# Start of a transformer-step kernel reordered: conv constants, modulation loads and bias tables on other places of their queues

## The chip, the cores and the metric

The kernel runs on one core of one Trainium2 chip. The metric is device microseconds of one execution, as the median of several runs. TensorE (PE in the rows) does the matmuls, VectorE (DVE), ScalarE (ACT) and GpSimd (POOL) work beside it, and SyncE (SP) issues nearly all DMAs. Each engine works through its own instructions in a fixed order.

## The reference

One layer of a streaming encoder step, on 2048 prompt rows and 8 x 16 sample rows of width 1024. Two head groups run side by side on one projection:

```python
sh1, sc1, g1, sh2, sc2, g2 = modulation(c, w_mod, b_mod)      # silu(c) @ w_mod + b_mod, in six parts
h = rmsnorm(x, norm1_g) * (1 + sc1) + sh1
proj = h @ w_in
o_a, conv_state, s = mixer_a(proj, conv_left, s0, conv_w, ...)  # conv of width 4 on q/k/v, gated delta rule
qb = rmsnorm(proj[..., QB:KB], qn_g); kb = rmsnorm(proj[..., KB:VB], kn_g); vb = proj[..., VB:]
o_b = band attention of qb, kb, vb with rel_bias on clipped distances
x = x + g1 * (concat(o_a, o_b) @ w_out)
h = rmsnorm(x, norm2_g) * (1 + sc2) + sh2
x = x + g2 * (relu(h @ w_up) ** 2 @ w_down)
```

w_mod is 1024 x 6144; all is float32. Before a row of x can be projected, the parts shift1 (section 0) and scale1 (section 1) of the modulation must be known.

## The kernel before

Each product is made of three matmuls (`mm3`, L160): a value is split into a high part, rounded to fp32r, and a low part, the rest. `weights` (L166) loads a tile of a weight matrix into a buffer `raw` (three of them), lets ScalarE cast it into the high half of a buffer `w` (four of them, L175), and GpSimd subtract to get the low half (L180). For w_in in the first block of rows the low half is then stored in DRAM (s_w_in, L183), and each later block loads it from there (L178) instead of subtracting.

Phase 1 goes over six blocks of rows: block 0 is two prompt tiles of 128 rows and the sample tile, blocks 1 to 4 have three tiles, block 5 two. `proj_a` makes of each block the gates of group A (PSUM tile psg; two loads of w_in, L0 and L1 in the prediction), then q, k, v (psq; one load of w_in for each of 12 sections, 24 matmuls of up to 384 columns), then the other half of the gates. `proj_b` makes q, k, v of group B (psb, 12 loads). Between them small steps of the delta rule are put in as fill; the projection of group B for blocks 5, 4 and 2 comes last, with the first attention block as fill. Phase 2 is attention, w_out, w_up and w_down.

Ahead of block 0 stands `modulation_start` (L220). It loads sections 1 and 0 of w_mod in 16 pieces of 512 KB through nine buffers raw0, sums each with `mod_mm` (psum tile mps), adds b_mod, and turns the sum by a matmul with `sel` (ptm) into the columns modT. On the way it loads the three x tiles of block 0, each after four sums. After its loop come `conv_consts` (three pairs of small loads, 24 transposes) and `load_hT`, which normalises x, transposes it (psh), scales it with modT and splits it into hT, the input of all projections. hT's columns 0 to 511 need quarters 0 and 1 of the sections only, the others quarters 2 and 3.

The other four sections of w_mod are 32 pieces, one loaded by `mod_step` (L272) after each q/k/v section from block 1 on; so they are loaded in blocks 1, 2 and two thirds of 3. `rel_bias` (L1090) writes the reversed bias table s_ext to DRAM and copies it out to s_bias (8 x 128 rows of 640 floats) and s_bs, from DRAM to DRAM; s_bias is first read by the attention behind block 5.

All DMAs named here stand in SyncE's one queue. The order on each engine is not the order of the code: a list scheduler places each instruction when the program is built, in each engine's order, and the chip keeps to it.

## Time and profile before

| what | value |
|---|---|
| median of 3 runs | 3190.09 us (3189.9 to 3201.82) |
| the profiled execution | 3191.66 us |
| its span in the trace | 3190.0 us, 53098 instructions |
| PE busy | 3060.4 us (96%) |
| DVE, ACT, POOL busy | 1768.1, 1471.8, 593.5 us |
| block 0 (first gate matmul to the start of block 1) | 46 to 203 us |

The profile is of one execution. A busy PE is not PE at its peak, since matmuls overlap and their ends are modelled. In a timeline row the bracket at the end is the idle time of the engine before that instruction, and what released it.

### The profile page before, as it was taken

Reading aid. Unit: us, or ns where it says so; the run is one execution under the profiler, and the core shown is the slowest. Engines: PE = TensorE matmul, PEld = TensorE weight load, DVE = VectorE, ACT = ScalarE, POOL = GpSimd, SP = SyncE. Lnnn points to the kernel's source line nnn. Section 1 sums busy time; section 2 is a strip of 40 time slices with the busy share of each in tenths; the row PEclk is TensorE's granted clock in tenths of the full one; section 3 lists DMA queues with packets and bytes.
Section 4 is the critical chain, followed back from the end, with each engine's and each line's share of the span. In section 5 each row is a group of like instructions: output and inputs, shape, how many; then the busy total and the mean of one; then the engine's idle time right before and its main releaser. Section 6 shows DMA issues by size and latency. Waiting matters only on the chain. (4 is left out here: it accounts for less than half of the span.)

```text
span 3190.0 us, 53098 instructions
## 1 busy us (share of the span) xinstructions
PE 3060.4 (96%) x19649; PEld 2717.8 (85%) x19649; DVE 1768.1 (55%) x4358; ACT 1471.8 (46%) x2803; POOL 593.5 (19%) x495
## 2 busy tenths in 40 slices
PE   6999999999999989998999999999999999999998
PEld 5998988899989878887999988888988877888887
DVE  4775677777868664675256652444645433442223
ACT  3554545555556555545345453444355333333222
POOL 3631212120212347642222000000000000000000
PEclk8999999999989989998999999999999999999999
DMA  9799897888888768886777766666766667856664
GB/s 295 238 293 300 260 291 221 264 259 245 275 267 272 217 225 268 252 291 192 247 252 246 254 202 188 201 186 205 236 203 200 214 223 228 272 173 196 192 191 139
DMA packets 629116, 747.44 MB, mean 234 GB/s; under 512 B 59680, under 2 KB 483600, under 8 KB 626808
## 3 DMA queue, kind: packets, MB, share of 16 engines
q1 hardware_dynamic: 623096, 712.58, 70.6%
q0 software_dynamic: 5760, 31.46, 3.1%
q8 instruction: 155, 2.54, 0.3%
q14 instruction: 105, 0.86, 0.1%
HBM read 631.29 MB, written 115.52 MB: 234 GB/s over the span
## 5 line engine op out<-in xcount | busy, mean ns | idle before, releaser
L175 ACT CAST w<-raw 128x1024 fp32r<-128x1024 f32 (+1 forms) x528 | 552.0, 1046 | 381.8 <-PE psd L164 212.5
L1479 PE MATMUL psu<-hT,w 128*128 128x512 f32 (+2 forms) x1328 | 471.6, 357 | 4.8 <-ACT hT L104 4.4
L1480 PE MATMUL psu<-hT,w 128*128 128x512 f32 (+2 forms) x1328 | 470.9, 355 | 0.0
L1481 PE MATMUL psu<-hT,w 128*128 128x512 f32 (+2 forms) x1328 | 469.8, 354 | 0.7 <-DMA w<-s_w_up 0.7
L162 PE MATMUL psd<-w,u 128*128 128x512 f32 x1088 | 430.9, 396 | 0.4 <-DVE y L82 0.4
L164 PE MATMUL psd<-w,u 128*128 128x512 f32 x1088 | 429.7, 396 | 0.2 <-DVE u L82 0.2
L163 PE MATMUL psd<-w,u 128*128 128x512 f32 x1088 | 427.2, 393 | 1.8 <-POOL w L82 1.8
L82 POOL TENSOR_TENSOR w<-raw,w 128x1024 fp32r<-128x1024 f32 (+1 forms) x140 | 338.3, 2428 | 269.5 <-ACT w L175 184.5
L79 DVE SCALAR_TENSOR_TENSOR psu<-psu,r 128x512 f32<-128x512 f32 (+2 forms) x160 | 98.8, 617 | 408.1 <-ACT r L92 407.9
L82 DVE TENSOR_TENSOR y<-y,psd 128x512 f32<-128x512 f32 x238 | 162.5, 685 | 251.9 <-PE psd L164 250.6
L1479 PEld LDWEIGHTS psu<-hT,w 128*128 128x128 f32 x1328 | 251.1, 190 | 36.2 <-ACT hT L104 5.3
L1481 PEld LDWEIGHTS psu<-hT,w 128*128 128x128 f32 x1328 | 251.4, 189 | 32.8 <-DMA w<-s_w_up 1.0
L1480 PEld LDWEIGHTS psu<-hT,w 128*128 128x128 f32 x1328 | 251.7, 190 | 30.5 <-issue 0.8
L164 PEld LDWEIGHTS psd<-w,u 128*128 128x128 f32 x1088 | 204.3, 188 | 47.2 <-issue 0.8
L92 ACT ACTIVATE r<-psu 128x512 f32<-128x512 f32 (+2 forms) x160 | 85.4, 533 | 344.1 <-issue 201.8
L163 PEld LDWEIGHTS psd<-w,u 128*128 128x128 f32 x1088 | 204.8, 188 | 46.1 <-POOL w L82 2.2
L162 PEld LDWEIGHTS psd<-w,u 128*128 128x128 f32 x1088 | 204.5, 188 | 44.6 <-DVE y L82 1.0
L162 PE MATMUL psb<-w,hT 128*128 128x256 f32 x816 | 237.1, 291 | 0.3 <-ACT hT L104 0.3
L164 PE MATMUL psb<-w,hT 128*128 128x256 f32 x816 | 234.3, 288 | 2.4 <-DVE hT L82 1.8
L163 PE MATMUL psb<-w,hT 128*128 128x256 f32 x816 | 234.5, 288 | 0.0
L518 PE MATMUL psq<-hT,w 128*128 128x384 f32 (+1 forms) x576 | 195.9, 340 | 9.0 <-ACT ba L498 8.9
L519 PE MATMUL psq<-hT,w 128*128 128x384 f32 (+1 forms) x576 | 194.2, 337 | 0.0
(316 smaller groups left out, 6492.5 us busy)
## 6 DMA issues: line engine op xcount, KB each, us to landing
raw<-in_w_up_dram SPq DMA_DIRECT2D x160, 512.0 KB
raw<-in_w_down_dram SPq DMA_DIRECT2D x160, 512.0 KB
raw<-in_w_in_dram SPq DMA_DIRECT2D x156, 512.0 KB
w<-s_w_in SPq DMA_DIRECT2D x130, 512.0 KB
w<-s_w_down SPq DMA_DIRECT2D x128, 512.0 KB
w<-s_w_up SPq DMA_DIRECT2D x96, 512.0 KB
raw<-in_w_out_dram SPq DMA_DIRECT2D x40, 512.0 KB
x<-in_x_prompt_dram SPq DMA_DIRECT2D x38, 512.0 KB
```

The source lines that it names most:

```text
L79: (eng or self.nc.vector).scalar_tensor_tensor(out, in0, scalar, in1, op0, op1)
L82: (eng or self.nc.vector).tensor_tensor(out, in0, in1, op)
L92: self.nc.scalar.activation(out, in_, func, **kw)
L162: mm(out, lh, rh, start=first, stop=False)
L163: mm(out, lh, rl, start=False, stop=False)
L164: mm(out, ll, rh, start=False, stop=last)
L175: nc.scalar.copy(w[:, 0, 0:n], r)
L518: mm(pc, wh, hT[:, k, 0, 0:T], start=(k == 0), stop=False)
L519: mm(pc, wh, hT[:, k, 1, 0:T], start=False, stop=False)
L1479: mm(ps[:, c0:c1], wh, h2[:, k, 0, c0:c1], start=(k == 0), stop=False)
L1480: mm(ps[:, c0:c1], wh, h2[:, k, 1, c0:c1], start=False, stop=False)
L1481: mm(ps[:, c0:c1], wl, h2[:, k, 0, c0:c1], start=False, stop=(k == KT - 1))
```

## The change

Five things are moved.

1. In `modulation_start` the conv rows are loaded right behind the first two w_mod pieces, in two loads instead of six; x tiles are loaded after each fourth w_mod piece; there are ten buffers raw0 and two more pieces go into free `big` buffers. The 12 conv transposes on 28 rows each (24 before, on 4 or 24 rows) are made after eight sums.
2. The turn of a summed row into modT (`finish`) comes one quarter of a section later than its sum, and as soon as two quarters of both sections are there, half of hT is made for all three tiles (`load_aq`, `load_bq`); `load_hT` is gone.
3. s_bias and s_bs are issued from GpSimd's queue.
4. The 32 later w_mod loads are spread over the 60 q/k/v sections of blocks 1 to 5.
5. In block 5 (`mix`) every second w_in tile gets its low part by subtraction again, not from DRAM.

```diff
@@ -36,7 +36,7 @@
 NT2 = max(len(b) for b in BLOCKS2)
 LATE = (4, 2)
 GP = 3
-NPRE = 9
+NPRE = 10
 
 
 def bcast(ap, axis, n):
@@ -174,11 +174,12 @@
         nc.sync.dma_start(r.rearrange("p (a b) -> p a b", a=a), src)
         nc.scalar.copy(w[:, 0, 0:n], r)
         key, kept = (name, k0, c0), self.s_w[name]
-        if key in self.stored:
+        self.turn += self.mix
+        if key in self.stored and not (self.mix and self.turn % 2):
             nc.sync.dma_start(w.bitcast(F32)[:, 1, 0:n], kept[self.stored[key]][:, 0:n])
             return v(0), v(1)
         self.tt(w[:, 1, 0:n], r, w[:, 0, 0:n].bitcast(F32), ALU.subtract, eng=nc.gpsimd)
-        if self.keep[name]:
+        if self.keep[name] and key not in self.stored:
             m = sum(k[0] == name for k in self.stored)
             nc.sync.dma_start(kept[m][:, 0:n], w.bitcast(F32)[:, 1, 0:n])
             self.stored[key] = m
@@ -226,11 +227,22 @@
         crow = p0.tile([P, D], F32, name="crow")[0:R]
         nc.sync.dma_start(crow[0:1], i["c_prompt"])
         nc.sync.dma_start(crow[1:R], i["c_sample"])
-        load = lambda n: self.mod_load(*first[n], p0.tile([P, D], F32, tag="raw0", name="raw0", bufs=NPRE))
         rvs, xs = [], []
-        for n in range(min(NPRE, len(first))):
-            rvs.append(load(n))
+
+        def load(n):
+            pool, tag, bufs = (self.hp, "big", 2) if n in (NPRE, NPRE + 1) else (p0, "raw0", NPRE)
+            rvs.append(self.mod_load(*first[n], pool.tile([P, D], F32, tag=tag, name="raw0", bufs=bufs)))
+
+        for n in range(min(NPRE + 2, len(first))):
+            load(n)
+            if n % 4 == 3 and len(xs) < len(tiles):
+                x = self.hp.tile([P, D], F32, tag="x", name="x", bufs=self.nx)
+                nc.sync.dma_start(x, self.x_src(tiles[len(xs)]))
+                xs.append(x)
             if n == 1:
+                cwt = p0.tile([28, 1536], F32, name="cwt")
+                nc.sync.dma_start(cwt[0:24], i["state_conv"][0].rearrange("b w c -> (b w) c"))
+                nc.sync.dma_start(cwt[24:28], i["conv_w"][0])
                 gains = p0.tile([16, P], F32, name="gains")
                 nc.sync.dma_start(gains[0:8], i["norm1_g"][0].rearrange("(a b) -> a b", b=P))
                 nc.sync.dma_start(gains[8:16], i["norm2_g"][0].rearrange("(a b) -> a b", b=P))
@@ -252,22 +264,31 @@
         nc.tensor.transpose(pr[:, 0:16], gains, self.ident[0:16, 0:16])
         nc.vector.tensor_copy(self.rowT, pr[:, 0:16])
         order = list(dict.fromkeys(c[0] for c in first))
+        xs = [self.normed(x, t) for x, t in zip(xs, tiles)]
+        done = []
+
+        def finish():
+            sec, q, row = done.pop(0)
+            self.mod_finish(sec, q, row, self.gp, "g")
+            if sec == first[-1][0] and q % 2:
+                for j, t in enumerate(tiles):
+                    self.load_bq(j, q // 2, self.load_aq(t, xs[j], 0, 1, q // 2))
+
         for n, (sec, q, u) in enumerate(first):
-            if n + NPRE < len(first):
-                rvs.append(load(n + NPRE))
-            if n % 4 == 3 and len(xs) < len(tiles):
-                x = self.hp.tile([P, D], F32, tag="x", name="x", bufs=self.nx)
-                nc.sync.dma_start(x, self.x_src(tiles[len(xs)]))
-                xs.append(x)
             if u == 0:
                 ps = self.gp.tile([P, 512], F32, tag="g", name="mps")[:, 0:256]
             self.mod_mm(ps, rvs[n], u, u == 0, u == 1)
+            if n == 7:
+                self.conv_consts(cwt)
+            if n + NPRE + 2 < len(first):
+                load(n + NPRE + 2)
             if u:
                 row = rows[:, order.index(sec), q * 256:(q + 1) * 256]
                 self.tt(row, row, ps, ALU.add)
-                self.mod_finish(sec, q, row, self.gp, "g")
-        self.conv_consts(p0)
-        return xs
+                done.append((sec, q, row))
+                if len(done) > 1:
+                    finish()
+        finish()
 
     def mod_step(self):
         if self.mod_todo:
@@ -328,41 +349,37 @@
-    def load_hT(self, tiles, xs, sh, sc):
-
-        for j, t in enumerate(tiles):
-            xn = self.normed(xs[j] if xs else None, t)
-            self.load_b(j, self.load_a(t, xn, sh, sc))
-            self.fill_step()
-
     def load_a(self, t, xn, sh, sc):
-        nc = self.nc
-        tmps = []
-        for q in range(2):
...
+        return [self.load_aq(t, xn, sh, sc, q) for q in range(2)]
+
+    def load_aq(self, t, xn, sh, sc, q):
...
     def load_b(self, j, tmps):
-        cs = slice(j * P, (j + 1) * P)
         for q, tmp in enumerate(tmps):
-            ks = slice(4 * q, 4 * q + 4)
-            self.split(self.hT[:, ks, 0, cs], self.hT[:, ks, 1, cs], tmp)
+            self.load_bq(j, q, tmp)
+
+    def load_bq(self, j, q, tmp):
+        cs, ks = slice(j * P, (j + 1) * P), slice(4 * q, 4 * q + 4)
+        self.split(self.hT[:, ks, 0, cs], self.hT[:, ks, 1, cs], tmp)
@@ -436,25 +453,21 @@
         self.act(self.alog, self.alog, AF.Exp)
         self.ts(self.alog, self.alog, -1.0, ALU.mult)
 
-    def conv_consts(self, p0):
-        nc, c, i = self.nc, self.p1, self.i
+    def conv_consts(self, t):
+        nc, c = self.nc, self.p1
 
         self.cw = c.tile([P, 12, 4], F32, name="cw")
         self.hist = c.tile([P, 12, 3], F32, name="hist")
         nc.vector.memset(self.hist, 0.0)
         self.hists = c.tile([P, 12, NB * 3], F32, name="hists")
-        for g in range(3):
-            gs = slice(g * 512, (g + 1) * 512)
-            t = p0.tile([24, D], F32, tag="cwt", name="cwt", bufs=3)
-            w4, h24 = t[0:4, 0:512], t[0:24, 512:1024]
-            nc.sync.dma_start(w4, i["conv_w"][0][:, gs])
-            nc.sync.dma_start(h24, i["state_conv"][0].rearrange("b w c -> (b w) c")[:, gs])
+        for g in range(6):
+            gs = slice(g * 256, (g + 1) * 256)
             ps = self.pa.tile([P, 512], F32, tag="pa", name="psc")
-            for k in range(4):
-                nc.tensor.transpose(ps[:, k * 4:(k + 1) * 4], w4[:, k * P:(k + 1) * P], self.ident[0:4, 0:4])
-                nc.tensor.transpose(ps[:, 64 + k * 24:64 + (k + 1) * 24], h24[:, k * P:(k + 1) * P], self.ident[0:24, 0:24])
-            self.ts(self.cw[:, 4 * g:4 * g + 4], ps[:, 0:16].rearrange("p (k r) -> p k r", r=4), 0.5, ALU.mult)
-            nc.vector.tensor_copy(self.hists[:, 4 * g:4 * g + 4], ps[:, 64:160].rearrange("p (k r) -> p k r", r=24))
+            for k in range(2):
+                nc.tensor.transpose(ps[:, k * 28:(k + 1) * 28], t[0:28, gs.start + k * P:gs.start + (k + 1) * P], self.ident[0:28, 0:28])
+            pv = ps[:, 0:56].rearrange("p (k r) -> p k r", r=28)
+            self.ts(self.cw[:, 2 * g:2 * g + 2], pv[:, :, 24:28], 0.5, ALU.mult)
+            nc.vector.tensor_copy(self.hists[:, 2 * g:2 * g + 2], pv[:, :, 0:24])
 
     def conv(self, y, pre, c, n, sub=None):
         for j in range(4):
@@ -536,7 +549,8 @@
                 self.act(ps[:, 0:T], y[:, 0:T], AF.Tanh)
                 self.stt(dst[:, 0:T], ps[:, 0:T], 1.0, y[:, 0:T], ALU.add, ALU.mult)
                 self.later(lambda c=c, dst=dst: self.qkv_out(c, dst, tiles, ssq, ssk))
-                if self.bi:
+                self.slot += self.bi > 0
+                if self.bi and self.slot * 32 // 60 > (self.slot - 1) * 32 // 60:
                     self.mod_step()
         self.flush()
         gates(0)
@@ -1039,8 +1053,8 @@
             self.nx, self.nA, self.inplace = 3, 4, True
             self.hT = self.p1.tile([P, KT, 2, self.nt * P], F32R, name="hT1")
             with tc.tile_pool(name="p0", bufs=1, side="right") as p0:
-                xs = self.modulation_start([(sec, q, u) for q in range(4) for sec in (1, 0) for u in range(2)],
-                                           BLOCKS1[0], p0)
+                self.modulation_start([(sec, q, u) for q in range(4) for sec in (1, 0) for u in range(2)],
+                                      BLOCKS1[0], p0)
             self.mod_todo = [(sec, q, u) for sec in (2, 3, 4, 5) for q in range(4) for u in range(2)]
             self.tp = R_("p1t")
             self.cp = pst.enter_context(tc.tile_pool(name="p1a", bufs=1, side="right"))
@@ -1052,13 +1066,13 @@
             ca = lambda b: 24 * (512 + 1536) * len(B[b])
             cb = lambda b: 24 * 1536 * len(B[b])
             last = len(B) - 1
-            self.load_hT(B[0], xs, 0, 1)
             for bi, tiles in enumerate(B):
                 self.bi = bi
                 self.keep["w_in"] = bi == 0
                 if bi == 1:
                     self.rel_bias()
                 self.drain_to(bi - 2)
+                self.mix = bi == last
                 blk = self.proj_a(tiles, self.hT, B[bi + 1] if bi in LATE else ())
                 if bi == last:
                     break
@@ -1076,6 +1090,7 @@
             rest = [last] + list(LATE)
             self.pace(0.85 * sum(cb(b) for b in rest))
             for b, nb in zip(rest, rest[1:] + [None]):
+                self.mix = b == last
                 self.proj_b(B[b], self.hT, B[nb] if nb is not None else ())
             self.drain()
             nc.sync.dma_start(self.o["gdn_prompt"][0, 0].rearrange("h k v -> k h v"), self.S)
@@ -1095,8 +1110,8 @@
         nc.vector.tensor_copy(rev[:, EXT - 64 - REL:EXT - 64], ext[:, ::-1])
         nc.vector.tensor_copy(rev[:, 0:EXT - 64 - REL], bcast(ext[:, REL - 1], 1, EXT - 64 - REL))
         nc.sync.dma_start(self.s_ext, rev)
-        nc.sync.dma_start(self.s_bias, dram_ap(self.s_ext, P, [[EXT, BH], [-1, P], [1, 640]]))
-        nc.sync.dma_start(self.s_bs, dram_ap(self.s_ext, P, [[EXT, BH], [-1, SL], [1, 528]]))
+        nc.gpsimd.dma_start(self.s_bias, dram_ap(self.s_ext, P, [[EXT, BH], [-1, P], [1, 640]]))
+        nc.gpsimd.dma_start(self.s_bs, dram_ap(self.s_ext, P, [[EXT, BH], [-1, SL], [1, 528]]))
 
     def softmax(self, ap, ps, bias, n):
 
@@ -1555,6 +1570,7 @@
     def run(self):
         self.nraw, self.nw = 3, 4
         self.deferred, self.lanes, self.pending, self.fill_rate, self.fill_acc = [], ([], [], []), [0, 0, 0], 0.0, 0.0
+        self.slot, self.mix, self.turn = 0, False, 0
         self.front, self.solved, self.spent = 0, 0, 0
         self.constants()
         self.phase1()
```

SyncE's order ahead of block 0. Before (raw with a number is a w_mod piece, raw from in_w_in the first weights of block 0):

```order
L281 DMA raw_189<-in_w_mod_dram 128x4x256
L434 DMA alog<-in_a_log_dram 128x4
L281 DMA raw_196<-in_w_mod_dram 128x4x256
L435 DMA dtb<-in_dt_bias_dram 128x4
L174 DMA raw<-in_w_in_dram 128x4x264 x2
L174 DMA raw<-in_w_in_dram 128x8x128
L1093 DMA ext<-in_rel_bias_dram 8x320
L281 DMA raw_207<-in_w_mod_dram 128x4x256
```

The last piece of w_mod stands behind the first three loads of w_in. After, at the same place:

```order
L240 DMA x<-in_x_sample_dram 128x1024
L302 DMA raw_204<-in_w_mod_dram 128x4x256
L302 DMA raw_210<-in_w_mod_dram 128x4x256
L302 DMA raw_218<-in_w_mod_dram 128x4x256
L302 DMA raw_224<-in_w_mod_dram 128x4x256
L443 DMA gdng<-in_gdn_norm_g_dram 128x1
L446 DMA qkg<-in_qn_g_dram 128x64
L447 DMA qkg<-in_kn_g_dram 128x64
L451 DMA alog<-in_a_log_dram 128x4
L452 DMA dtb<-in_dt_bias_dram 128x4
L174 DMA raw<-in_w_in_dram 128x4x264 x2
L174 DMA raw<-in_w_in_dram 128x8x128
```

All of w_mod and the third x tile now stand ahead of w_in. GpSimd's order in block 0, before (r is the small power of a row's norm):

```order
L82 TENSOR_TENSOR w<-raw,w 128x1056 x2
L82 TENSOR_TENSOR w<-raw,w 128x1024
L295 MEMSET mrow 128x256
L101 TENSOR_TENSOR r<-r,cpow 128x1
L82 TENSOR_TENSOR w<-raw,w 128x1024
L101 TENSOR_TENSOR r<-r,cpow 128x1
L82 TENSOR_TENSOR w<-raw,w 128x1024 x3
```

The low parts follow one another with nothing but small steps between. After:

```order
L82 TENSOR_TENSOR w<-raw,w 128x1056
L316 MEMSET mrow 128x256
L82 TENSOR_TENSOR w<-raw,w 128x1056
L82 TENSOR_TENSOR w<-raw,w 128x1024
L1113 DMA s_bias<-s_ext 1024x1x640
L1114 DMA s_bs<-s_ext 128x1x528
L101 TENSOR_TENSOR r<-r,cpow 128x1
L82 TENSOR_TENSOR w<-raw,w 128x1024
L101 TENSOR_TENSOR r<-r,cpow 128x1
```

The two table copies stand between the low part of the third load and that of the fourth. GpSimd's order in block 5, after (before, no subtraction of w stands here; nk and rq are the key and query norms of the block, X a value tile of the delta rule):

```order
L316 MEMSET mrow 128x256
L82 TENSOR_TENSOR w<-raw,w 128x1024
L82 TENSOR_TENSOR X<-X,nk 128x512
L101 TENSOR_TENSOR zs<-zs,cpow 128x4
L82 TENSOR_TENSOR w<-raw,w 128x1024
L82 TENSOR_TENSOR ta<-low_434,g 128x512
L82 TENSOR_TENSOR w<-raw,w 128x1024
L316 MEMSET mrow 128x256
L82 TENSOR_TENSOR w<-raw,w 128x1024
L101 TENSOR_TENSOR nk<-ssk,cpow 128x8
L82 TENSOR_TENSOR w<-raw,w 128x1024
```

Recomputed low parts stand behind the X product and behind the block's own key norms.

## Rows read from the trace of the kernel before

**Rows 1.** The page: busy time; PE busy tenths in 40 slices

```profile
PE 3060.4 (96%) x19649; PEld 2717.8 (85%) x19649; DVE 1768.1 (55%) x4358; ACT 1471.8 (46%) x2803; POOL 593.5 (19%) x495
...
PE   6999999999999989998999999999999999999998
```

**Rows 2.** Windows: length; PE, PEld, DVE, ACT, POOL busy; clock; DMA; GB/s

```profile
0.00:4.00 4.00, 0.00 (x0) 0.00 (x0) 1.74 (x7) 0.71 (x1) 3.36 (x14) 1.00 0.31 93
4.00:28.00 24.00, 16.51 (x121) 9.56 (x121) 10.23 (x29) 4.11 (x5) 7.03 (x21) 1.00 1.08 341
28.00:32.00 4.00, 4.00 (x26) 2.41 (x25) 1.47 (x8) 1.15 (x1) 0.55 (x1) 1.00 0.48 131
...
52.00:68.00 16.00, 14.84 (x97) 14.16 (x96) 7.86 (x17) 6.29 (x12) 5.34 (x3) 1.00 0.73 258
...
80.00:100.00 20.00, 19.20 (x116) 18.78 (x115) 16.77 (x43) 11.55 (x37) 11.71 (x7) 0.97 0.70 209
...
71.00:81.30 10.30, 3.80 (x12) 3.80 (x13) 6.72 (x20) 5.79 (x18) 4.12 (x3) 0.50 0.96 308
```

**Rows 3.** Timeline of SyncE's DMA issues: start, duration, line, transfer

```profile
35.56 0.57 SPq L281 DMA_DIRECT2D raw<-in_w_mod_dram  x1
...
43.74 0.29 SPq L1097 DMA_DIRECT2D s_ext<-ext  x1
...
47.62 2.70 SPq L1098 DMA_DIRECT2D s_bias<-s_ext  x1
50.37 7.84 SPq L1099 DMA_DIRECT2D s_bs<-s_ext  x1
...
60.38 0.38 SPq L174 DMA_DIRECT2D raw<-in_w_in_dram  x1
```

**Rows 4.** Timeline of PE: start, duration, line, operation, idle time before

```profile
26.29 0.30 PE L455 MATMUL psc<-ident,cwt 24*128 24x24 f32 x1
...
42.30 1.08 PE L287 MATMUL mps<-raw,cT 128*32 128x256 f32 x8 [2.86 <-DMA raw<-in_w_mod_dram]
...
46.41 0.57 PE L162 MATMUL psg<-w,hT 128*128 128x264 f32 x1
...
64.18 0.34 PE L518 MATMUL psq<-hT,w 128*128 128x384 f32 x1
...
77.50 0.69 PE L518 MATMUL psq<-hT,w 128*128 128x384 f32 x1 [8.95 <-ACT ba L498]
```

**Rows 5.** Timeline of ScalarE, same columns

```profile
73.25 1.04 ACT L175 CAST w<-raw 128x1024 fp32r<-128x1024 f32 x1 [7.67 <-DMA raw<-in_w_in_dram]
```

**Rows 6.** DMA issues of the first 70 us: transfer, queue, count, KB each

```profile
raw<-in_w_mod_dram SPq DMA_DIRECT2D x16, 512.0 KB
...
s_bias<-s_ext SPq DMA_DIRECT2D x1, 2560.0 KB
```

**Rows 7.** GpSimd: its timeline; its DMA issues of L1136 (ns, min/median/max)

```profile
80.06 2.40 POOL L82 TENSOR_TENSOR w<-raw,w 128x1024 fp32r<-128x1024 f32 x1
...
L1136 POOL DMA_DIRECT2D KV<-s_kv x8: 530/608/762, 879.8 to 1040.3; - x8
```

**Rows 8.** Windows of blocks 1 to 5, columns as in rows 2

```profile
200.00:300.00 100.00, 99.55 (x764) 88.32 (x762) 62.77 (x171) 51.59 (x120) 4.63 (x7) 1.00 0.98 306
...
400.00:500.00 100.00, 94.21 (x718) 81.77 (x717) 71.77 (x206) 42.64 (x97) 15.35 (x15) 0.95 0.96 296
500.00:600.00 100.00, 98.76 (x670) 89.51 (x670) 84.73 (x253) 52.84 (x123) 14.99 (x16) 0.99 0.77 236
...
900.00:1000.00 100.00, 95.19 (x804) 89.90 (x803) 70.57 (x233) 59.44 (x134) 24.04 (x28) 0.88 0.73 225
...
802.00:863.00 61.00, 56.76 (x447) 55.45 (x446) 49.49 (x167) 34.52 (x89) 9.65 (x9) 0.94 0.91 282
```

**Rows 9.** What GpSimd waited for, 802 to 965 us: total, times, longest

```profile
POOL nk L101 <- DVE ssk L87: 27.1, 1, 27.1
...
POOL X L82 <- DMA X<-s_vt: 21.4, 4, 11.1
```

33 lines of the change are left out of this document (16 added, 17 removed).

## The prediction

> **What bounds the kernel now.** I read the page first: TensorE is busy 96% of the span, so only its idle time, some 130 us, and its slow-clock stretches can be won. The slices show where they lie: PE stands at 6 tenths in the first slice and at 8 or 9 from there on [rows 1]. So I cut the first 100 us finer [rows 2]. From 4 to 28 us the DMA engines are full (share 1.08, 341 GB/s) and PE works in small pieces: the start waits for bytes. Two holes follow in which the DMA engines are not full although PE still waits for data: 28 to 32 us (0.48) and 52 to 68 us (0.73). From 71 to 81.3 us PE is busy 3.80 of 10.3 us at a granted clock of 0.50; after 80 us it is busy 19.2 of 20, so from there on it is PE's own work.
>
> Then SyncE's queue, to see what the holes are [rows 3]. The last w_mod load of the start is issued at 35.56, behind the first w_in loads and rel_bias. At 47.62 and 50.37 the two bias-table copies s_bias and s_bs hold the queue 2.70 and 7.84 us, and the next w_in load goes out only at 60.38. PE's rows give the price [rows 4]: that last w_mod piece is summed at 42.30 after a DMA wait of 2.86 us, the first gate matmul starts at 46.41, and before the third q/k/v weight load PE stands still 8.95 us until 77.50. What releases it is ScalarE's ba copy; ScalarE in turn was held 7.67 us, until 73.25, by the cast whose raw tile (the one issued at 60.38) had not landed [rows 5].
>
> **Part by part.** I name the w_in loads of block 0 L0, L1 (gates), L2, L3, L4 (q/k/v) and work out when L4's matmuls start: before, 77.50.
>
> *w_mod, x and conv rows ahead of w_in; ten plus two buffers.* By the order all 16 w_mod loads and three x loads now go out before the first w_in load. The bytes are the same: 16 + 3 loads of 512 KB (0.524 MB) are 9.96 MB [rows 6], small tensors about 0.3 MB. With 0.37 MB by 4 us (93 GB/s) and then 341 GB/s [rows 2], 10.26 MB land at 4 + 9.89/0.341 = 33 us, if the hole at 28 us is gone: in the order nothing stands between these loads that waits for conv rows. From the last w_mod sum to the first gate matmul takes 46.41 - 42.30 = 4.1 us [rows 4], so 37.1. L0 (128 x 1056 floats, 0.54 MB) lands 1.6 us behind w_mod at 34.6; its cast is 1.04 [rows 5] and GpSimd's subtraction 2.40 [rows 7], so 38.0. Gates start at about 38, 8 us earlier.
>
> *From there to L4.* The 24 matmuls of L3 ran from 64.18 to 77.50 - 8.95 = 68.55 [rows 4], 0.182 us each for 384 columns, so 0.125 for a gate's 264. PE needs 72 gate and 48 q/k/v matmuls: 9.0 + 8.7 = 17.7 us. For a half-speed stretch like the one from 71 to 81.3, worth up to 5 us, I add 4, as PE is still stopping often there. 38.0 + 17.7 + 4 = 59.7.
>
> *Biases on GpSimd's queue.* SyncE no longer stands 10.5 us; who stands now is GpSimd, and behind it in its order are a small power operation and the subtraction of L3. No row shows a 1024-row copy on that queue. The nearest are the KV loads it issues (128 rows, median 608 ns [rows 7]) and SyncE's own 2.70 + 7.84. So 1.2 to 10.5 us; issuing cannot take less than nothing, so it is no gain for GpSimd. GpSimd is done with L0 to L2 at 38.0 + 2 x 2.4 = 42.8; it waits for s_ext, which I put at 46 (issued at 43.74 before, [rows 3]). With the power and the subtraction, 3 us, L3's low half is there between 50.2 and 59.5. PE wants it at 38.0 + 9.0 + 4 + 4.4 = 55.4: late by 0 to 4.1 us. I take 2, nearer to the KV rows because they are of the same queue. L4 then starts at 61.7: a gain of 16.
>
> *The tables' bytes.* They are 2560 KB [rows 6] and, for 128 rows of 528 floats, 264 KB: 2.9 MB, 8.5 us of DMA at 341 GB/s, and they now run beside L4 to L7 instead of stopping them. 0 to 8.5 us come back later; I take 4, since after 80 us the DMA engines have room (share 0.70). On the other side the clock stood at 0.50 until 81.3 [rows 2]: 3.8 us at half speed after 77.50, 1.9 us more to win. 16 + 1.9 - 4 = 14 us.
>
> *Sums a quarter later, rows by halves, conv transposes.* 12 transposes replace 24, two loads replace six. All of this lies before 46 us beside the DMA engines' full stretch, so zero; if that cover were gone, 12 transposes of 0.30 us [rows 4] would show, 3.6 us.
>
> *Later w_mod loads over all blocks.* 32 loads in 32 of 60 slots instead of in the first 32: the sums on PE are the same number, and 13 loads (6.8 MB) move from blocks 1 to 3 into blocks 4 and 5. In 200 to 300 us, where they were thickest, the DMA engines are at 0.98 but PE is busy 99.55 of 100: nothing to win. In 400 to 500 PE is busy 94.21 at clock 0.95, against 98.76 at 0.99 in 500 to 600 [rows 8]; if thinner loads made the first like the second, 4.6 us idle and 4 us of clock would go. Taken: 0, between -8.6 and +8. The upper end is the clock: 900 to 1000 was granted 0.88, that is 24 us at half speed, 12 us lost, from short stalls; a rearranged order can add most of such a stretch.
>
> *Half of the last block's low parts recomputed.* 14 subtractions of 2.40 us [rows 7], 34 us on GpSimd, which in the first 61 us of that block is busy 9.65 [rows 8]; and 14 loads (7.3 MB) fewer for the DMA engines, which about pays for the seven w_mod loads that come in. If GpSimd is ahead of PE this is 0; its danger is the last rival.
>
> Sum: 14 us off. The steps are made against the profiled execution, 3190.0 us span and 3191.66 us in all; the median of the runs, 3190.09, is 1.6 us below it and gets the same 14: **3176 us**, with its own range 3169 to 3183. A measurement of this kernel tells about 0.5% (16 us, below 3174 or above 3206) from no change.
>
> **The rivals.** *Only the holes close: 3183.* If the first 80 us are bound by bytes wherever they are queued, only the two holes come back: (1.08 - 0.48)/1.08 x 4 = 2.2 us and, against the same full share, (1.08 - 0.73)/1.08 x 16 = 5.2 us, 7 us. For it: a share of 0.96 even from 71 to 81.3, right at the stall. Against it: much of what landed by 77 us (s_bias, the next block's x rows) isn't what L4 waits for. The Trainium skill, DMA: Bandwidth & Descriptors, "Issuing engines are not separate DMA queues", points the same way: transfers of all issuing engines run on the same 16 DMA engines, and another issuer saves only issue time. No run here shows it yet for this pair.
>
> *The later stages gain too: 3168.* 14 us plus the 8.6 us of 400 to 500 us. For it: the DMA share there is 0.96, and thinner loads shorten what chains of small steps wait for. Against it: 200 to 300 has the same share and no stall.
>
> *GpSimd held long by the tables: about 3193.* If writing the 1152 rows takes GpSimd much longer than SyncE's 10.5 us, every low half of block 0 from L3 on is late. At 25 us, L3's low half comes at 46 + 25 + 3 = 74, L4 starts at about 79 and, with the 4 us above less the 1.9, the start ends 3 us behind the old one. For it: GpSimd makes all of block 0's low halves in turn. Against it: the KV rows' 0.6 us. The Trainium skill, SBUF — State Buffer, "A bandwidth-pool intuition that's wrong", has a DMA from GpSimd's queue that took 620 ns alone and 3100 ns beside a VectorE copy; an estimate from that factor of five on nine times 0.6 us is about 27 us. Whether it holds here no row shows.
>
> *The last block waits for GpSimd: slower, about 3204.* Between 802 and 965 us GpSimd's queue stands up to 27.1 us for ssk and 11.1 for an X tile [rows 9], and recomputed tiles now stand behind both. Four weight buffers at 12 tiles in 61 us, 5.1 us each, give about 15 us of lead: 27.1 + 11.1 - 15 = 23 us of PE waiting and 5 us of clock, less the 14. It decides once GpSimd's waits ahead of needed tiles pass 15 + 14 us. Against it: the long ssk wait ends when block 5's own q/k/v tiles are done, so few tiles are wanted in it.
>
> **How the numbers follow.** 3176: 42%. Holes only, 3183: 26%. Later stages too, 3168: 20%. GpSimd held, 3193: 6%. Slower, 3204: 6%. Below 3174 lie about four tenths of the first (16%), a little of the second (2%) and nearly all of the third (18%): 0.36. Above 3206 lie half of the last and a little of the one before: 0.05. The rest, 0.59, is within 0.5%. The range leaves out the tails of the outer cases: 3159 to 3197.
>
> **What would show it.** Right: the first gate matmul near 38 us and L4 near 62; no s_bias row on SyncE; 28 to 32 and 52 to 68 us at a DMA share near 1; the stages after 100 us as long as before. Wrong: a gap in GpSimd's subtractions of over 10 us behind the s_bias issue; L4's cast still waiting for its DMA at 70 us; PE waiting for GpSimd's w between 802 and 965 us; or new half-speed stretches after 200 us larger than the start's gain, which no step here can foresee.

## The result, and the profile after

The changed kernel takes **3211.62 us** (median of 6, 3205.56 to 3218.01) where the kernel before takes 3192.26 (3189.9 to 3206.73) beside it: a ratio of 1.0051, interval 1.0034 to 1.0069. It is slower by 16 us (11 to 22), just past what can be told from no change. The forecast was 3176, with a range of 3159 to 3197. The profiled execution took 3213.07 us, its span is 3211.4.

The page first (busy time; PE in 40 slices; answers [rows 1]):

```profile
PE 3066.5 (95%) x19637; PEld 2718.4 (85%) x19637; DVE 1802.9 (56%) x4364; ACT 1472.7 (46%) x2803; POOL 628.1 (20%) x511
...
PE   6999999999899989998999999999999999999998
```

GpSimd is busy 34.6 us longer than before, 14 subtractions' worth. VectorE is 34.8 us longer too, with only six instructions more. Nobody had moved work to VectorE.

The windows of the start (columns as in [rows 2]):

```profile
28.00:32.00 4.00, 3.82 (x29) 1.56 (x28) 3.54 (x8) 1.53 (x3) 0.00 (x0) 1.00 1.10 350
32.00:52.00 20.00, 18.47 (x116) 14.84 (x112) 17.07 (x37) 9.59 (x16) 10.63 (x8) 1.00 0.90 260
52.00:68.00 16.00, 10.57 (x63) 9.84 (x61) 7.40 (x11) 4.65 (x8) 6.76 (x5) 1.00 0.87 306
71.00:81.30 10.30, 3.64 (x11) 3.64 (x12) 7.75 (x24) 6.39 (x22) 3.26 (x2) 0.50 0.72 227
```

Both holes of the DMA engines are closed (0.48 became 1.10, 0.73 became 0.87), and PE has the same stop behind them at the same half clock (0.50). Its rows, first the gates' first matmul, then the third q/k/v load (L4), as in [rows 4]:

```profile
40.54 0.79 PE L162 MATMUL psg<-w,hT 128*128 128x264 f32 x2
...
77.66 0.69 PE L531 MATMUL psq<-hT,w 128*128 128x384 f32 x1 [14.58 <-ACT ba L511]
```

The gates start 5.9 us earlier and L4 at the same time: 77.66 against 77.50. ScalarE is again held by a cast whose raw tile has not landed ([rows 5]), now for 11.74 us, and SyncE, which no longer issues the tables, stands still in its own issues ([rows 3]); GpSimd issues both tables in 1.9 us:

```profile
70.20 1.04 ACT L175 CAST w<-raw 128x1024 fp32r<-128x1024 f32 x1 [11.74 <-DMA raw<-in_w_in_dram]
```

```profile
56.50 2.72 SPq L184 DMA_DIRECT2D s_w_in<-w  x1
59.32 1.59 SPq L174 DMA_DIRECT2D raw<-in_w_in_dram  x1
61.00 7.72 SPq L184 DMA_DIRECT2D s_w_in<-w  x1
```

```profile
48.57 1.28 POOL L1113 DMA_DIRECT2D s_bias<-s_ext  x1 [2.29 <-DMA s_ext<-ext]
49.85 0.62 POOL L1114 DMA_DIRECT2D s_bs<-s_ext  x1
```

The late tile is not L4's. It belongs to L5, the load behind it, issued at 49.81; L4's low half was done at 59.41. What PE needs for L4 is the PSUM buffer of the third gate tile (psg and psq share three), which ScalarE's ba copy reads last, and in ScalarE's order that copy stands behind the cast of L5 (L5's issue, L4's subtraction, the copy):

```profile
49.81 0.40 SPq L174 DMA_DIRECT2D raw<-in_w_in_dram  x1
```

```profile
57.00 2.40 POOL L82 TENSOR_TENSOR w<-raw,w 128x1024 fp32r<-128x1024 f32 x1 [1.20 <-issue]
```

```profile
77.44 0.17 ACT L511 COPY ba<-psg 128x8 f32<-128x8 f32 x1 [0.23 <-DVE sgw L79]
```

Where the rest went I read from all PE rows of a trace. For each matmul I take the time to the next one's start, less the 20th percentile of that time over all matmuls of its line, shape and tile (doubled where the granted clock is half). The rest is **stall**, and the doubling **slow clock**. What remains as PE's own work is 2771 to 2776 us in every kernel of this document, so differences lie in stall and slow clock, given together here by stage of the profiled execution (us). "L4 at" and "block 1 at" are the starts of the first q/k/v matmul of L4 and of block 1. "Chain" counts the matmuls of the key-key products (pkk, the delta rule's first step; 136 in all) that PE has done when block 4's q/k/v begin.

| kernel | time | ratio to before | L4 at | block 1 at | to L4 | rest of block 0 | blocks 1-3 | blocks 4, 5 q/k/v | from there to the end of attention's first block | chain |
|---|---|---|---|---|---|---|---|---|---|---|
| before | 3192.3 | | 77.5 | 210.7 | 41.8 | 12.3 | 78.1 | 20.8 | 75.3 | 96 |
| changed | 3211.6 | 1.0051 | 77.7 | 214.3 | 43.6 | 15.6 | 73.8 | 36.4 | 77.7 | 80 |
| start_only | 3196.1 | 1.0008 | 77.0 | 215.6 | 43.1 | 17.6 | 80.8 | 19.6 | 82.2 | 96 |
| no_mix | 3200.8 | 1.0019 | 78.3 | 216.4 | 44.4 | 17.2 | 73.8 | 41.6 | 74.4 | 80 |
| mix_only | 3195.5 | 1.0003 | 79.0 | 212.3 | 43.4 | 12.4 | 81.0 | 29.4 | 70.8 | 96 |
| spread_only | 3215.1 | 1.0074 | 78.8 | 211.5 | 43.2 | 11.8 | 74.8 | 34.2 | 85.5 | 80 |
| mix_other | 3213.4 | 1.0076 | 77.1 | 214.6 | 43.6 | 16.5 | 75.3 | 42.0 | 77.9 | 80 |
| shift_one | 3190.0 | 1.0005 | 78.3 | 214.5 | 42.7 | 15.2 | 76.5 | 20.6 | 72.3 | 96 |
| spread_1to4 | 3212.8 | 1.0076 | 79.3 | 213.0 | 43.7 | 12.8 | 76.1 | 34.9 | 78.3 | 80 |
| spread_1to3 | 3195.8 | 1.0016 | 75.8 | 211.2 | 40.2 | 14.4 | 84.7 | 21.4 | 76.0 | 96 |
| dense_then_late | 3195.9 | 1.0017 | 78.9 | 211.5 | 43.3 | 11.5 | 73.0 | 28.8 | 78.1 | 96 |
| start_late_tables | 3203.6 | 1.0042 | 63.5 | 203.1 | 29.1 | 18.5 | 96.1 | 19.0 | 76.6 | 96 |
| start_x_tables | 3200.8 | 1.0021 | 62.6 | 202.6 | 28.6 | 19.0 | 103.3 | 19.4 | 76.1 | 96 |
| start_small_packets | 3192.4 | 0.9994 | 75.2 | 212.6 | 41.1 | 16.5 | 77.3 | 19.4 | 78.4 | 96 |
| tables_at_620 | 3188.3 | 0.9984 | 63.7 | 202.8 | 29.6 | 18.0 | 83.9 | 18.3 | 81.9 | 96 |

The changed kernel's loss is 15.6 us in blocks 4 and 5, 5 in the start and block 0, 2 behind, 5 in all that follows, less 4 won in blocks 1 to 3. Times of one kernel differ by 10 us and more from execution to execution, and a profile shows one of them (those of no_mix and start_only are the slowest of their ten runs, 7 and 8 us above the medians); the ratios carry the verdicts, the stages only where the difference is larger than that between kernels of the same kind.

### The profile page after: what moved, and what is told of

Read it like the earlier page. It is cut to its first block, busy times and chain, and to the rows that moved or that the text cites. A ratio compares the mean times of both kernels' runs of the same rounds, so it can differ in the third digit from the quotient of the medians.

```text
span 3211.4 us, 53078 instructions
## 1 busy us (share of the span) xinstructions
PE 3066.5 (95%) x19637; PEld 2718.4 (85%) x19637; DVE 1802.9 (56%) x4364; ACT 1472.7 (46%) x2803; POOL 628.1 (20%) x511
## 4 chain that ended last, share of the span: by engine, by line
PE 70%; DMA 12%; DVE 8%; ACT 3%; issue 2%; POOL 1%; SPq 1%; ACTq 0%; POOLq 0%; DVEq 0%
PE psu L1494 7%; PE psu L1495 7%; PE psu L1496 7%; PE psd L164 7%; PE psd L162 7%; PE psd L163 7%; DMA raw<-in_w_in_dram 2%; PE psS L1280 2%; PE pv L1298 2%; PE psP L1288 2%; PE pso L162 1%; PE pso L163 1%; DVE y L79 1%; DMA raw<-in_w_up_dram 1%; PE pso L164 1%
## 5 line engine op out<-in xcount | busy, mean ns | idle before, releaser
L175 ACT CAST w<-raw 128x1024 fp32r<-128x1024 f32 (+1 forms) x528 | 552.5, 1047 | 415.2 <-PE psd L164 210.7
L82 POOL TENSOR_TENSOR w<-raw,w 128x1024 fp32r<-128x1024 f32 (+1 forms) x154 | 371.7, 2425 | 315.4 <-ACT w L175 220.6
L1496 PEld LDWEIGHTS psu<-hT,w 128*128 128x128 f32 x1328 | 251.3, 189 | 34.6 <-POOL w L82 2.3
L92 ACT ACTIVATE r<-psu 128x512 f32<-128x512 f32 (+2 forms) x160 | 85.5, 534 | 341.4 <-issue 199.7
```

What stands on the lines that cost most here:

```text
L82: (eng or self.nc.vector).tensor_tensor(out, in0, in1, op)
L92: self.nc.scalar.activation(out, in_, func, **kw)
L175: nc.scalar.copy(w[:, 0, 0:n], r)
L1496: mm(ps[:, c0:c1], wl, h2[:, k, 0, c0:c1], start=False, stop=(k == KT - 1))
```

## Experiments

**1. The parts alone.** My first theory (A) was that the recomputed low parts cost the time; its rival (B), the new order as a whole. no_mix drops the mix, start_only the spread as well:

```diff
-                self.mix = bi == last
...
-                self.mix = b == last
...
-                self.slot += self.bi > 0
-                if self.bi and self.slot * 32 // 60 > (self.slot - 1) * 32 // 60:
+                if self.bi:
```

mix_only puts the mix alone into the kernel before, spread_only the spread alone.

> The changed kernel, but the last block loads all its stored low parts again (no subtraction on GpSimd). Theory A, the 14 subtractions of the last block cost the time (the two traces differ by 17 to 25 us between 800 and 990 us): about 3190 to 3196, level with the kernel before, and the stage from the start of block 5 to the end of its delta rule within 5 us of the length before. Theory B, the new order of instructions as a whole costs the time, wherever it lies: 3207 to 3216, as the changed kernel.

> The changed start alone: no recomputed low parts, and the 32 later w_mod loads in the first 32 slots as before. Theory A: what the start brings, -3 to +4 us against the kernel before (the third q/k/v load began at 77.66 us against 77.50). If the spread w_mod loads are worth anything, this is slower than no_mix by that, at most 8 us. Theory B: 3200 to 3215.

> The kernel before with the 14 recomputed low parts of the last block and nothing else of the change. Theory A: 3203 to 3213, 12 to 22 us slower than the kernel before, all of it between 800 and 1000 us. Theory B, the mix is harmless and the loss comes from the rest: 3187 to 3195.

> The kernel before with the later w_mod loads spread over all five blocks and nothing else. Theory A: 0 to 8 us faster than the kernel before (blocks 1 to 3 gained about 8 us in the changed kernel), 3182 to 3190. Rival: seven more loads in block 5 collide with its own, where the DMA engines are 0.9 busy: 3195 to 3205.

Measured: no_mix 1.0019 (0.9999 to 1.0039), start_only 1.0008 (0.9992 to 1.0024), mix_only 1.0003 (0.9987 to 1.0019), spread_only 1.0074 (1.0045 to 1.0103). Theory A falls: the mix alone costs nothing in the end, though 8.6 us more stall in blocks 4 and 5. The part that I had put at nothing, the spread, costs 24 us alone (14 to 33). And the parts do not add up: with the changed start the spread costs 3 to 4 us, less than these runs can tell from nothing, and the mix on top of both about 10 (the intervals of no_mix and of the changed kernel still touch). Why the spread costs 24 us beside the old start and 4 beside the new one, no run shows.

**2. Is it the luck of the order?** Each edit makes the scheduler place everything anew. shift_one does the same work as before, one slot later; mix_other is the changed kernel with the other half recomputed.

```diff
-                if self.bi:
+                self.slot += self.bi > 0
+                if self.slot > 1:
                     self.mod_step()
```

```diff
-        if key in self.stored and not (self.mix and self.turn % 2):
+        if key in self.stored and not (self.mix and self.turn % 2 == 0):
```

> The kernel before with its 32 later w_mod loads one slot later (slots 2 to 33 of 60): the same work, bytes and stages, only the scheduler's order comes out another way. Theory A, the loads in blocks 4 and 5 cost the time: level with the kernel before, within 4 us. Theory C, each reshuffled order has its own luck, whatever was edited: anywhere from 3188 to 3215, and if it lies over 8 us from the kernel before, single edits can't be priced by single kernels.

> The changed kernel with the other half of the last block's low parts recomputed (every second one, begun one later): 13 or 14 subtractions, the same stages. Theory A: like the changed kernel, 3207 to 3217. Theory C, the order's luck: over 8 us away from the changed kernel, most likely lower, 3194 to 3204.

Measured: 1.0005 (0.9987 to 1.0024) and 1.0076 (1.0061 to 1.0091). Theory C finds no support: this new order costs nothing, and the changed kernel's variant is as slow as it is or slower. Two orders do not rule luck out for others.

**3. What in the spread costs.** First the places: blocks 1 to 4 alone (`32 // 48` for `32 // 60`). Then the 13 loads and sums that fall into blocks 4 and 5, left out one by one and together. The names say what stays: late_neither, which is shown, has neither, late_loads_alone keeps the loads, and late_sums_alone keeps the sums and feeds them from columns of hT where `None` stands:

```diff
+            bi = self.bi
+            if bi < 4:
                 rv = self.mod_load(*c, self.hp.tile([P, D], F32, tag="x", name="rawx", bufs=self.nx))
+            else:
+                rv = None
...
+        if rv is not None:
             ps = self.pa.tile([P, 512], F32, tag="pa", name="mps")[:, 0:256]
             self.mod_mm(ps, rv, u, True, True)
             self.tt(row, row, ps, ALU.add)
```

> The kernel before with the later w_mod loads spread over blocks 1 to 4 only (32 of 48 slots), none in block 5. Theory A, the seven loads in block 5 cost the time of spread_only: 3190 to 3198, and block 5 as long as before. Theory A2, the loads in block 4 cost as much, where the last block's first delta-rule steps are: 3203 to 3212. Theory C: anywhere from 3188 to 3215.

> spread_only, with the 13 w_mod loads that fall into blocks 4 and 5 left out, and their matmuls and adds with them (so part of the modulation is not computed). TensorE's own work falls by 13 times about 0.9 us, 12 us. Theory D1, the loads or the sums in blocks 4 and 5 make the stalls there: TensorE's stalls and slow clock from the first q/k/v of block 4 to the last of block 5 fall from 34 us to the 19 to 21 of kernels without the spread; total 3186 to 3192. Theory D2, the thinner sums in blocks 1 to 3 let the scheduler put the delta-rule chain later, and the stalls follow from that: they stay at 33 to 41 us and only the work goes; total 3200 to 3204.

> spread_only, with the 13 loads in blocks 4 and 5 kept and only their 52 matmuls and 13 adds left out. If the loads (bytes, buffers, SyncE's queue) make the stalls: 33 to 41 us of stall in that stretch, 3200 to 3204. If the sums do: 19 to 21 us, 3186 to 3192. D2 expects 33 to 41 us here as in the other two of this group.

> spread_only, with the 13 loads in blocks 4 and 5 left out and their matmuls and adds kept, fed from columns of hT (so the sums are of other data). If the loads make the stalls: 19 to 21 us in that stretch, 3198 to 3203. If the sums do, or by D2: 33 to 41 us, 3211 to 3216.

Measured: spread_1to4 1.0076 (1.0059 to 1.0092), with 11.5 us of it in block 4's q/k/v, so the loads in block 5 are not the cause. late_neither, late_loads_alone and late_sums_alone: 3204.06, 3199.15 and 3200.03 us, and 31.9, 32.9 and 33.8 us of stall and slow clock in blocks 4 and 5, against 34.2 in spread_only; their chain stands at 72, 80 and 72. By that stretch D2 holds: what stands there does not depend on the loads or sums there. By the totals it does not: they fell by 11 to 16 us, more than the left-out work (4 us by the rows, not the 12 that I expected), and late_sums_alone, which does all of that work, is 11 us below the least that D2 expected. So the late loads and sums seem to cost something outside that stretch, and these runs don't locate it. Part of the spread's price may lie behind block 5 (10 us in the row of spread_only), but that column can't carry it: start_only, which loses nothing, has 7 us more there too.

What all kernels with the thin spread share is in the last column of the table. Windows of the key-key products alone (length, PE busy and count, PEld, DVE; then the clock, DMA share and GB/s of the window), up to block 4's q/k/v and from there to block 5's last, in the changed kernel, in start_only and in dense_then_late, the next experiment:

```profile
0.00:701.90 701.90, 20.40 (x80) 14.22 (x80) 18.41 (x60) 0.98 0.85 262
701.90:876.00 174.10, 9.56 (x40) 7.21 (x40) 9.68 (x31) 0.97 0.79 229
```

```profile
0.00:717.30 717.30, 24.20 (x96) 16.94 (x96) 22.38 (x72) 0.97 0.85 265
717.30:869.20 151.90, 6.15 (x24) 4.08 (x24) 5.69 (x18) 0.99 0.85 261
```

```profile
0.00:703.50 703.50, 24.14 (x96) 17.07 (x96) 20.87 (x68) 0.97 0.84 262
703.50:865.80 162.30, 6.16 (x24) 4.10 (x24) 7.01 (x23) 0.99 0.89 267
```

With the w_mod loads thinned out ahead of it, the scheduler's order starts the q/k/v of block 4 before the delta rule of block 3 is as far: 16 of 96 products, and the chain behind them, are done beside block 4's and 5's own. It is not the number of loads: dense_then_late has the same 13 fewer ahead of block 4, at the old pace, and keeps its 96. Two kernels keep the chain in place. dense_then_late has 19 loads at the old pace and 13 in blocks 4 and 5; spread_1to3 has `32 // 36`.

```diff
-                if self.bi:
+                self.slot += self.bi > 0
+                if 0 < self.slot <= 19 or self.bi >= 4 and (self.slot - 36) * 13 // 24 > (self.slot - 37) * 13 // 24:
                     self.mod_step()
```

> The kernel before with 19 of the later w_mod loads in slots 1 to 19, one in each, and the last 13 in blocks 4 and 5. In the scheduler's order all four key-key products of block 3's tiles (pkk) stand ahead of block 4's q/k/v, as in the kernel before; in spread_only 16 of 96 stand behind. Theory O, the order of the delta-rule chain makes the stalls in blocks 4 and 5: 19 to 23 us from the first q/k/v of block 4 to the last of block 5, 3190 to 3198. Theory L, late loads and sums make them: 32 to 41 us, 3203 to 3213.

> The kernel before with the 32 later w_mod loads in 32 of the 36 slots of blocks 1 to 3: none in block 4 or 5, sums a little thinner, and by the order the chain of block 3 is ahead of block 4 as before (though behind at block 3's start, as in spread_only). Theory O: 19 to 23 us of stall in that stretch, 3188 to 3196. If being behind at block 3's start is enough: 30 us or more there, 3200 to 3212.

Measured: 1.0017 (1.0001 to 1.0033) and 1.0016 (0.9996 to 1.0037), with 28.8 and 21.4 us in blocks 4 and 5. dense_then_late has the same late loads as spread_only and is 18 us faster by the ratios, so the late loads are at most a small part of the price (dense_then_late costs 5 us, 0 to 11). But its 28.8 us are 6 more than theory O allowed, and of the 18 us only 5 lie in blocks 4 and 5, 7 behind them and the rest further on. mix_only shows that stalls in that stretch can come from elsewhere too. Every whole kernel with the chain at 80 has 34 to 42 us there, every one with it at 96 has 18 to 29. That is a pattern over the fifteen kernels of the table and no proof: the chain's place can't be set by itself, the five kernels with it at 80 are just the five whose loads are spread over 48 or 60 sections, and no_mix has it at 80 and loses only 6 us.

**4. What the tables cost.** start_late_tables calls `rel_bias` ahead of block 3. start_x_tables leaves the call at block 1 and takes an x buffer, which holds it to 200 us:

```diff
-                if bi == 1:
+                if bi == 3:
                     self.rel_bias()
```

```diff
-        x = self.hp.tile([P, D], F32, tag="big", name="ext", bufs=2)
+        x = self.hp.tile([P, D], F32, tag="x", name="ext", bufs=self.nx)
```

> start_only with rel_bias called ahead of block 3 instead of block 1, so that the tables' 2.9 MB leave the first 100 us. Theory A, the tables' bytes on the DMA engines hold back the w_in loads of block 0: the stall of 14.5 us before the third q/k/v load shrinks to under 4 us, that load starts at 62 to 67 us instead of 77, and the time falls by 8 to 14 us, to 3182 to 3188. Theory B, the stall comes from the order on ScalarE and SyncE and not from the bytes: that load still starts after 74 us and the time stays at 3194 to 3198.

> start_only with rel_bias in an x buffer, which is free only when block 1's x rows are used, so that the tables are written about 200 us and not in block 2 or 3 as in start_late_tables. Theory A, the stall before the third q/k/v load is the tables' bytes and they cost little at 200 us: that load at 63 to 64 us, 3181 to 3187. Rival, the tables cost about as much wherever they run, since the DMA engines are 0.98 busy from 200 to 300 us: load at 63 us, but 3193 to 3203.

L4 starts at 63.5 and 62.6 us with no stall ahead of it, and block 1 12.5 and 13.0 us earlier than in start_only: the forecast of 61.7 was the start without the tables. Yet the times are 1.0042 (1.0027 to 1.0057) and 1.0021 (1.0004 to 1.0038): blocks 1 to 3 have 15 and 22 us more. In start_late_tables some 7 of the 15 lie in the last part of block 2, where the tables' rows land (484 to 499 us), and 6 in the last part of block 3, over 80 us behind, which no run ties to the tables. In start_x_tables 20 of the 22 lie at one place, where the same stop as in the changed kernel is seen. GpSimd issues s_bias at 203.74, and then SyncE's issues of w take 5 to 7 us each and PE stops (SyncE, then PE):

```profile
209.25 4.69 SPq L179 DMA_DIRECT2D w<-s_w_in  x1
214.03 1.65 SPq L174 DMA_DIRECT2D raw<-in_w_in_dram  x1
215.78 6.66 SPq L179 DMA_DIRECT2D w<-s_w_in  x1
```

```profile
225.05 0.69 PE L531 MATMUL psq<-hT,w 128*128 128x384 f32 x1 [10.72 <-ACT ba L511]
```

The DMA records show why bytes worth 8.5 us hold the loads for 15. One part could have been read before: in the kernel before, s_bias is copied on SyncE's queue with nothing beside it, and from 56 to 60 us its rows land at 0.41 MB in 2 us, 205 GB/s and not 341; all 2.62 MB take from 54 to 67 us. The other part is what the loads get while it runs. Packets and MB that ended in 2 us, counted in the trace of start_only and of the kernel below:

```
start_only            GpSimd's queue    SyncE's queue
  60 to 62 us           74, 0.38 MB      193, 0.16 MB
  62 to 64 us           73, 0.37 MB      501, 0.25 MB
  64 to 66 us           75, 0.38 MB       75, 0.04 MB
  66 to 68 us           75, 0.38 MB       73, 0.04 MB
  70 to 72 us            0               932, 0.63 MB
start_small_packets
  62 to 64 us          275, 0.44 MB      269, 0.14 MB
  64 to 66 us          238, 0.50 MB      235, 0.18 MB
```

From 64 to 68 us the two queues move one packet each in turn, and the tables' packets are 5120 bytes against 512 of SyncE's rows there. SyncE's queue has 0.04 MB in 2 us while that lasts, and 0.63 once the tables are done. From 60 to 64 us it still gets more packets through than GpSimd's; why, the records do not show. The Trainium skill, DMA: Bandwidth & Descriptors, "Queues, rings and completion order", says that a DMA engine goes round its queues packet by packet; the trace agrees, 75 to 75 and 238 to 235. start_small_packets writes the big table in five copies of 128 columns:

```diff
-        nc.gpsimd.dma_start(self.s_bias, dram_ap(self.s_ext, P, [[EXT, BH], [-1, P], [1, 640]]))
+        for a in range(0, 640, P):
+            nc.gpsimd.dma_start(self.s_bias[:, :, a:a + P], dram_ap(self.s_ext, P + a, [[EXT, BH], [-1, P], [1, P]]))
```

> start_only with the big table written in five copies of 128 columns (512 bytes a row) on GpSimd's queue instead of one of 640 columns. Theory P, the two queues take turns packet by packet, so that GpSimd's 5120-byte packets starve SyncE's 512-byte rows: SyncE's queue keeps half of the rate or more while the tables run, the stall ahead of the third q/k/v load falls from 14.5 us to 3 to 7, that load starts at 65 to 70 us; 3184 to 3191 in all, and the tables take longer to land. Theory Q, bytes alone: stall 12 to 16 us, the load at 75 to 78 us, 3194 to 3199. If five issues hold GpSimd long (5 times 1.3 us), its subtraction for that load is late by up to 3 us in either case.

Measured: 0.9994 (0.9973 to 1.0015). The stall fell from 14.33 us (start_only, first row) to 9.57 and stands one load earlier:

```profile
76.97 0.69 PE L531 MATMUL psq<-hT,w 128*128 128x384 f32 x1 [14.33 <-ACT ba L511]
```

```profile
68.71 0.69 PE L531 MATMUL psq<-hT,w 128*128 128x384 f32 x1 [9.57 <-ACT ba L511]
```

L4 starts at 75.2 where 65 to 70 was expected. Theory P has the direction, not the size: the tables' packets still held 1.6 to 2.1 KB on average (0.44 MB in 275, 0.50 in 238; nearly all bytes in packets of 4096), and SyncE stood 15.93 us in three issues:

```profile
52.76 15.93 SPq L512 DMA_DIRECT2D s_sg<-sgw  x3
```

Then pieces on SyncE's own queue between the loads of block 0, with the changed start and with the old one (eight pieces of 64 rows of two heads, each pair behind a one-column operation):

```diff
+            r = self.rev[32:32 + BH, 0:1]
+            self.stt(r, y[32:32 + BH, 0:1], 0.0, r, ALU.mult, ALU.add)
+            nc.sync.dma_start(self.s_ext[k:k + 2], self.rev[32 + k:34 + k, 0:EXT])
...
+            nc.sync.dma_start(self.s_bias[j:j + 2, a:a + 64], dram_ap(self.s_ext, P + j * EXT - a, [[EXT, 2], [-1, 64], [1, 640]]))
```

> start_only with the tables written on SyncE's queue in pieces of 328 KB between the weight loads of block 0 (slots 3 to 11), each held by a one-column operation on VectorE that reads that slot's convolution. From 80 to 140 us the DMA engines of start_late_tables are 0.73 busy and TensorE is full, so there is room for about 5 MB. Theory A: the third q/k/v load at 63 to 64 us, block 1 begins at 203 to 206 us, no new stall in blocks 1 to 3: 3179 to 3186. Rival, 2.9 MB cost 10 to 15 us wherever they go: 3192 to 3200.

> The kernel before, with its own start, and the tables in the same pieces. Theory A: the 9 us stall ahead of the third q/k/v load goes, that load at 67 to 70 us, 3180 to 3186; the difference to start_pieces, 0 to 6 us, is what the reordered start is worth by itself. Rival: 3190 to 3196, if the tables cost the same in pieces.

Both failed: 1.0126 (1.0099 to 1.0154) and 1.0145 (1.0111 to 1.0179). L4 starts at 62.7 and 68.9 as expected, but the rest of block 0 has 52.5 and 53.3 us of stall and slow clock. I had counted bytes and not the queue: in start_pieces SyncE waited 9.7 us for s_ext to land ahead of the pieces, 3.6 for the holding operation and 19 for results of the convolution that now stood in another place, with every weight load behind.

Last, the tables in one go on SyncE's queue in block 3's b stage, held by an operation on that stage's first result of the second half:

```diff
+        if (self.bi, sec, half, j) == (3, 1, 1, 0):
+            self.bias_out(raw)
```

> start_only with the tables written in one go on SyncE's queue in block 3's b stage, about 620 us, held there by a one-column operation that reads that stage's first result of the second key half. Theory A, the tables cost nothing where the DMA engines have room (0.71 to 0.74 busy) and up to three weight loads are ahead: third q/k/v load at 63 to 64 us, block 1 begins at 203 to 206 us, stalls of block 3 within 4 us of start_only; 3179 to 3187 in all. Rival, 2.9 MB in one go stop the weight loads for 10 us there too: 10 us of stall in block 3, 3190 to 3197.

Measured: 3188.33 us, 0.9984 (0.9965 to 1.0004), with L4 and block 1 13 us earlier than in start_only, and blocks 1 to 3 3.1 us above it. Three of SyncE's issues take 8.6 us here as well, but PE works through that up to 640 us and idles 3.4 behind (windows of 40 us, columns as above, with ACT and POOL):

```profile
627.75 0.73 SPq L1118 DMA_DIRECT2D s_bias<-s_ext  x1
628.58 4.68 SPq L1026 DMA_DIRECT2D s_kv<-kTs  x1
633.31 3.22 SPq L1119 DMA_DIRECT2D s_bs<-s_ext  x1
```

```profile
600.00:640.00 40.00, 40.00 (x434) 37.57 (x433) 24.43 (x79) 22.06 (x48) 11.78 (x10) 1.00 0.75 248
640.00:680.00 40.00, 36.64 (x307) 36.43 (x306) 26.08 (x79) 18.21 (x41) 12.53 (x13) 0.96 0.96 316
```

It is the fastest kernel here, 8 us below start_only by the ratios, but its interval reaches 1: that it beats the kernel before is likely and not shown.

## Why the prediction was wrong

The forecast was 14 us faster, the result is 16 us slower. Of these 30 us the start accounts for 17 (start_only is 3 us slower where 14 faster was forecast), the spread and the mix, both put at 0, for the other 13.

*w_mod first, gates at 38.* Right in kind: no hole at 28 us, first gate at 40.54, 2.5 us late.

*GpSimd's issue, 2 us.* Right: 1.9 us, and the subtraction behind it starts at 52.45. The rival that held GpSimd long was wrong in its cause: GpSimd was held 1.9 us, not 25. That its 79 us for L4 lies near the measured 77.66 is luck. The rule of the Trainium skill cited with "only the holes close" (DMA: Bandwidth & Descriptors, "Issuing engines are not separate DMA queues"), that another issuer saves issue time alone, agrees with these rows (L4 at 77.66 against 77.50).

*The tables' bytes, 4 us.* This step failed. I let them run beside L4 to L7 and bounded them by 8.5 us at the full rate. The rows of s_bias alone landed over 13 us in the kernel before, and over 14 us here. It runs beside the weight loads, and at the worst SyncE's queue gets a small packet for a large one: L5, issued at 49.81, held ScalarE until 70.20. The sum followed L4's own weights, which were ready in time (59.41), and left out the path over ScalarE's order, though the kernel before shows it too: there the cast at 73.25 is that of L6, two loads behind L4. So L4 started at 77.66, not at 61.7; the 16 us of the start went, and with them the 1.9 us of clock. start_late_tables shows that without them the sum up to L4 would have held (63.5). Whether the ba copy ahead of that cast would have saved the stall with the tables in place, no run tried. But they must be written somewhere: at 200 us they cost 20, at 490 between 7 and 15, at 620, where weight loads lie ahead, about 3 by the same stages.

*Conv transposes and sums, 0.* Nothing in the traces speaks against it.

*w_mod spread, 0 with -8.6 to +8.* This failed by more than its range: 24 us alone. I asked what the loads and sums cost where they go, and the answer to that was about right (dense_then_late). I didn't ask what happens to the fill when work leaves blocks 1 to 3. The early blocks did gain (2 to 4 us of stall), and blocks 4 and 5 lost 13 to 21. What fits best is that the chain that gets less time in the early blocks is paid for there; it is not shown, and the rest of the 24 us stays open.

*Half of the low parts, 0.* By itself right in the total (1.0003), in company about 10 us, whose place is open: by the table no_mix has more stall in blocks 4 and 5 (41.6 us) than the changed kernel (36.4). The rival named GpSimd's w as what PE would wait for between 802 and 965 us. The longest wait there is another; PE waits for VectorE:

```profile
826.44 1.83 PE L857 MATMUL pS<-w,kt 128*128 128x128 f32 x7 [5.78 <-DVE w L82]
```

```profile
822.87 2.82 DVE L82 TENSOR_TENSOR E<-E,incl 128x512 f32<-128x512 f32 x1
825.62 1.27 DVE L82 TENSOR_TENSOR w<-pY,b 128x512 f32<-128x512 f32 x2
```

```profile
822.67 2.48 POOL L82 TENSOR_TENSOR w<-raw,w 128x1024 fp32r<-128x1024 f32 x1 [0.66 <-ACT w L175]
```

E takes 0.68 us elsewhere (median of its seven between 200 and 700 us); beside the subtraction it took 2.82 and ended 0.54 after it, as if it had waited for all of it. That is 2.1 of the 5.8 us that PE stood, one case and not the whole 10. (The 14 loads saved are also twice the seven that come in, where I had them about equal.)

*The chances.* Slower was given 5%, most of it from one mechanism in one block. That a scheduler places everything anew stood only in the upper end of the spread's range (+8): three edits, each put at nothing or better, came to 16 us more.

## What to carry to other kernels

Ask of a transfer moved to another queue which packets it puts between those of the loads that are needed next and how fast its own rows landed so far, and move it to where loads lie ahead of their use, not to where the engines have room on average. A late load can stop an engine that does not need it yet, through the order of a third: look at what stands behind its first use there. When work is moved out of a stage that also carries fill, look in the order of the engine where the fill ends up; its place may cost more than the work. Take an edit costed at nothing on the idle engine only after looking at which engine stands while it works.

## What the runs showed of the hardware

Two busy queues took turns packet by packet, whatever the packets' size (start_only, 64 to 66 us: 75 of 5120 bytes against 75 of about 0.5 KB; not so from 60 to 64). SyncE, issuing meanwhile, stood in the issue itself: 7.72 us for one, in start_small_packets 15.93 for three. The copy of s_bias from DRAM to DRAM moved 0.41 MB in 2 us with nothing beside it.

A VectorE operation with two inputs in SBUF can be held until a GpSimd subtraction beside it ends: E took 2.82 us for 0.68, and in the kernel before `qraw` times `ss` (128x256) 2.61 us, the median of five beside a subtraction, for 0.42. One that takes an input from PSUM was not held (E from pkk and E, 128x256: 0.41 us with and without). Over a run 14 subtractions (34 us of GpSimd) made VectorE busy 27 us longer (mix_only 1795.2 against 1768.1, the changed kernel 1802.9 against 1775.0 in no_mix). The Trainium skill, SBUF — State Buffer, "Who interferes with whom", says that a VectorE instruction with two SBUF inputs contends with a GpSimd instruction that reads SBUF, over a shared port pair that is locked exclusively; these rows agree.
